# Seven products of halves in place of eight, for two blocks of the gate and up product of each feed-forward layer

## The chip, the core and the metric

The kernel runs on one NeuronCore of a Trainium2 chip, as one launch. The metric is device time in microseconds (us): the median of the timed executions of the whole program. The core has five engines with a queue each: PE (TensorE, matrix products into PSUM), DVE (VectorE), ACT (ScalarE), POOL (GpSimd) and SP (SyncE, which issues the loads). Each works off its own instructions in the order in which the program lists them, and waits on semaphores for the others.

## The reference

A two-layer encoder for 256 tokens of width 1024 in fp32. Each layer is a feed-forward block, a mixer, and a second feed-forward block, all with RMSNorm ahead of them; so there are four feed-forward blocks (FFN) with two different mixers between them. The part that the change touches is the first product of each FFN:

```python
def swiglu(h, w_gu, w_down):
    g, u = jnp.split(h @ w_gu, 2, axis=-1)
    return (jax.nn.silu(g) * u) @ w_down

x = x + 0.5 * swiglu(rmsnorm(x, ffn1_norm[l]), ffn1_w_gu[l], ffn1_w_down[l])
```

Here h is 256 x 1024, w_gu is 1024 x 5632 (2816 gate columns and 2816 up columns) and w_down is 2816 x 1024.

## The kernel before, in words

**Precision.** Every fp32 operand of a product is split into two fp32r halves, hi (the rounded value) and lo (the rest), and a product is three matmul terms: hi by hi, hi by lo, lo by hi. The activations are split once (`xs`, lines 567 and 576-579). The weights are split as they come in: `fetch` (480-498) loads 1 MB (128 x 2048 fp32) into one of RAW = 4 buffers `raw`, and for each of its two parts of 1024 columns ACT copies it to `hi` (`E.copy`, which the planner may give to DVE) and DVE subtracts, `lo = raw - hi`. The parts live in a ring of RING = 6 pairs of hi and lo buffers: a part can be split only when the PE is done with the part six before it. 1024 columns of 128 rows are here called a **part**, of 1 MB two.

**The FFN** (`ffn`, 656-695). The 2816 hidden columns are 22 tiles of 128. A **pass** (672-679) computes two tiles: their two gate and two up products over K = 1024 in eight steps, 32 calls of `wide` (182-187), with the weights stationary and the 256 tokens moving. One `wide` is a matmul of 512 moving columns (both halves of the activations against hi) and one of 256 (their hi half against lo). A pass uses four parts of weights and 64 matmuls, into four PSUM banks, and 11 passes make the gate and up product. `evac` (661-669) then empties each tile's two banks: it adds the halves, multiplies by the row of 1/rms (`rb`), applies SiLU, multiplies gate by up, and splits the result into `hs`, tile by tile: for each tile 3 ACT copies or activations and a split, and on DVE four 256-wide instructions besides a 512-wide one. `hs` is the moving operand of the down product (682-695), with eight output tiles over 22 steps.

**The order of the work.** The program is recorded as a list of operations and put in order by a planner (`schedule`, 162-272), which keeps a clock for each engine, uses written costs (lines 308, 312, 318-321, 340), and of the operations that are ready on an engine takes the one with the lowest priority number. That number is the PE time recorded so far less a lead: 10e3 ns for weight splits (`LEAD_W`), 20e3 for evacuations (`LEAD`), 30e3 for loads (line 485). The resulting order is fixed in the program. In the profile nearly every instruction therefore has one line, that of the planner's emitter (L285 before, L289 after).

Of the kernel before, what the change touches and what calls it, by code (L numbers as in the profile page):

```python
# [14 lines left out]
AF = mybir.ActivationFunctionType  # L15
ALU = mybir.AluOpType
# [3 lines left out]
P = 128  # L20
# [18 lines left out]
LEAD, LEAD_A, LEAD_W = 20e3, 20e3, 10e3  # L39
PATIENCE = 500.0  # L40
WARM = 8


GC = {"norm": 0, "cq": 48, "bs": 51, "sub": 59, "mq": 60, "mk": 61}
# [307 lines left out]
def trunk_kernel(ctx: ExitStack, tc: tile.TileContext, a: dict, out: bass.AP):  # L352
# [108 lines left out]
    def load(ap, widths):  # L461

        o, ids = 0, []
        for w in widths:
            pieces.append((len(loads), o, w))
            ids.append(len(pieces) - 1)
            o += w
        loads.append((ap, o))
        return ids

    def first(raw, w, n):

        for k in range(4):
            o = NGC + (4 * n + k) * N
            c = slice(o if o > NGC else 0, o + N)
            Q.dma_start(out=gx[:, c], in_=a["gx"][:, c])
            c = slice(512 * k, 512 * k + 512)
            Q.dma_start(out=raw[:, c], in_=w[:, c])

    def fetch(n):  # L480
        while len(ready) <= min(n, len(pieces) - 1):
            d, o, w = pieces[len(ready)]
            while len(raws) <= d:
                ap, wide = loads[len(raws)]
                raw = raws_(SUB)
                with lead(30e3):
                    if len(raws) < 2:
                        first(raw, ap, len(raws))
                    else:
                        Q.dma_start(out=raw[:, :wide], in_=ap)  # L490
                raws.append(raw)
            hi, lo = his(PIECE), los(PIECE)
            cuts = 1 if len(ready) > 3 else 2
            with lead(LEAD_W):
                for c in (slice(z * w // cuts, (z + 1) * w // cuts) for z in range(cuts)):
                    E.copy(out=hi[:, c], in_=raws[d][:, o:o + w][:, c])
                    V.tensor_tensor(out=lo[:, c], in0=raws[d][:, o:o + w][:, c], in1=hi[:, c], op=ALU.subtract)
            ready.append((hi, lo))

    def weight(i):  # L500
        fetch(i)
# [41 lines left out]
    def dense(b, xh, xl, wh, wl, first, last):  # L543

        with prog.together():
            c = 0.0
            for l, r, s, e in ((xh, wh, first, False), (xh, wl, False, False), (xl, wh, False, last)):
                c += T.matmul(b, lhsT=l, rhs=r, start=s, stop=e)
# [20 lines left out]
    rr = [rr_[:, h:h + 1] for h in range(2)]  # L569

    def gains(n, j, w, k):

# [8 lines left out]
    def squares(k):  # L581

        if k == 0:
            S.activation(out=acc, in_=x[:, k, :], func=AF.Square)
            return
        sq = t1(N)
        S.activation(out=sq, in_=x[:, k, :], func=AF.Square)
        V.tensor_tensor(out=acc, in0=acc, in1=sq, op=ALU.add)

    def normed(n, k):  # L590

        scaled(n, k)
        squares(k)

    def rms():

# [56 lines left out]
    def finish(k):  # L653
        Q.dma_start(out=out[:, k, :], in_=x[:, k, :])

    def ffn(gu, dn, after):
        hs = Arena(region)(FT, 2, N)
        with lead(LEAD):
            rms_along()

        def evac(j, g, u):
            h, sg = t2(2, N), t1(N)
            for i, b in enumerate((g, u)):
                E.copy(out=h[:, i, :], in_=b[:, 1, :])
                V.tensor_tensor(out=h[:, i, :], in0=b[:, 0, :], in1=h[:, i, :], op=ALU.add)
            V.tensor_tensor(out=h, in0=h, in1=rows(rb, 2), op=ALU.mult)
            S.activation(out=sg, in_=h[:, 0, :], func=AF.Silu)
            V.tensor_tensor(out=sg, in0=sg, in1=h[:, 1, :], op=ALU.mult)
            split(hs[:, j, 0, :], hs[:, j, 1, :], sg)


        for j in range(0, FT, 2):
            banks = [bank(2, N) for _ in range(4)]
            for k in range(KT):
                for t in range(4):
                    wide(banks[t], *chunk(gu, 16 * j + 4 * k + t), xs[:, k], k == 0, k == KT - 1)
# [339 lines left out]


    def ffn_loads(i):
        gu = [n for s in range(FT) for n in load(a["gu"][i, s], (1024, 1024))]
        dn = [n for s in range(FT // 2) for n in load(a["dn"][i, s], (1024, 1024))]  # L1020
        return gu, dn

# [26 lines left out]
        for k in range(KT):  # L1049
            squares(k)  # L1050
    setup()
    ffn(*f10, norm[1])
    even(ev_in, ev_out, norm[2])
    ffn(*f20, norm[3])
    ffn(*f11, norm[4])
    odd(od_in, od_out, norm[5])
    ffn(*f21, finish)
    prog.emit(tc)


# [12 lines left out]

def _gate_up(w):

    return _chunks(w.reshape(KT, P, 2, FT // 2, 2, P).transpose(3, 0, 4, 2, 1, 5))


def _down(w, last):
# [78 lines left out]
```

## Time and profile before

| | |
|---|---|
| median of 3 timed runs | 947.79 us (947.37 to 948.18) |
| the profiled execution's own time | 947.75 us |
| its span in the trace | 946.0 us |
| PE, DVE, ACT busy share of the span | 99%, 77%, 58% |
| first FFN's gate and up product | from 5.26 us to 130.34 us |
| second FFN's gate and up product | starts at 288.27 us |
| bytes read from HBM | 165.86 MB |

How to read it: the trace is of one execution. Rows of a timeline give the start in us, the duration in us, the engine, and the operation with its operands by the program's names. Where the next instruction of an engine starts before the duration of the one ahead has passed, the two overlap in the engine's pipeline; the distance from start to start is then what an instruction costs in a queue that is never empty. A group row gives the count, the busy time and the mean duration, then the idle time of the engine just ahead of these instructions and what ended it.

### The profile page before, as it was taken

The page shows a single profiled execution, that of the slowest core. Times are in us where ns is not written, and L with a number is a line of the kernel's source. Part 1 is how long each engine was busy: PE and PEld are TensorE (multiplying, and loading weights), DVE is VectorE, ACT ScalarE, POOL GpSimd, SP SyncE. Part 2 cuts the span into 40 slices and gives each one's busy share as a digit, 9 for nine tenths or more (in the row PEclk, how much of TensorE's full clock was granted, in tenths as well). Part 3 has the DMA queues.
Part 4 walks back from the last instruction along what each step waited for, and adds up shares of the span by engine and source line. Part 5 has one row for each costly group of instructions (what it writes and reads, how often), then busy time and mean ns, then how long its engine had stood idle before and what let it go on. Part 6 is the DMA issues. An engine that isn't in the chain of part 4 may idle for free.

```text
span 946.0 us, 14528 instructions
## 1 busy us (share of the span) xinstructions
PE 939.6 (99%) x5564; PEld 827.1 (87%) x5564; DVE 724.0 (77%) x1326; ACT 548.4 (58%) x938; POOL 29.4 (3%) x57
## 2 busy tenths in 40 slices
PE   9999999999999999999999999999999999999998
PEld 8888888888899888888888888888989988888887
DVE  7997776579989878866588887756888698887642
ACT  7765655446856656554465656544587566565430
POOL 0920000000000000000000000000000000000000
PEclk9999999999999999999999999999999999999999
DMA  8675555543355555555555555554412355555520
GB/s 334 258 267 178 188 201 191 178 178 134 106 207 177 184 193 203 178 182 191 195 182 187 185 202 192 178 185 162 178 55 85 110 186 196 180 192 205 191 102 22
DMA packets 26422, 167.83 MB, mean 177 GB/s; under 512 B 2929, under 2 KB 5105, under 8 KB 7025
## 3 DMA queue, kind: packets, MB, share of 16 engines
q1 hardware_dynamic: 26352, 166.92, 50.0%
q8 instruction: 43, 0.70, 0.3%
q14 instruction: 27, 0.21, 0.1%
HBM read 165.86 MB, written 1.05 MB: 176 GB/s over the span
## 4 chain that ended last, share of the span: by engine, by line
PE 97%; DVE 1%; ACT 1%; DMA 0%; issue 0%; SPq 0%; ACTq 0%
PE bank L285 97%; DVE t L285 0%; ACT t L285 0%; DMA raw<-in_gu 0%; DVE sm L285 0%; ACT hi L285 0%; DVE region L285 0%; DVE lo L285 0%; ACT L285 0%; DVE hi L285 0%; DVE ssg L285 0%; DVE gx L285 0%; SPq L285 0%; DVE ssc L285 0%; DVE rc L285 0%
## 5 line engine op out<-in xcount | busy, mean ns | idle before, releaser
L285 DVE TENSOR_TENSOR lo<-raw,hi 128x1024 fp32r<-128x1024 f32 (+2 forms) x318 | 382.4, 1204 | 165.9 <-ACT hi L285 161.0
L285 ACT ACTIVATE hi<-raw 128x1024 fp32r<-128x1024 f32 (+3 forms) x310 | 322.6, 1043 | 306.1 <-PE bank L285 193.2
L285 PE MATMUL bank<-xs,hi 128*128 128x512 f32 x1408 | 490.8, 393 | 0.4 <-ACT hi L285 0.4
L285 PE MATMUL bank<-xs,lo 128*128 128x256 f32 x1408 | 394.8, 280 | 0.0
L285 PEld LDWEIGHTS bank<-xs,hi 128*128 128x128 f32 x1408 | 265.4, 189 | 59.1 <-ACT hi L285 0.7
L285 PE MATMUL bank<-region,hi 128*128 128x512 f32 (+1 forms) x982 | 296.6, 364 | 0.0
L285 PEld LDWEIGHTS bank<-xs,lo 128*128 128x128 f32 x1408 | 265.3, 188 | 0.7 <-DVE lo L285 0.7
L285 PE MATMUL bank<-region,lo 128*128 128x256 f32 x832 | 234.0, 281 | 0.0
L285 PEld LDWEIGHTS bank<-region,hi 128*128 128x128 f32 x982 | 174.9, 189 | 32.0
L285 PEld LDWEIGHTS bank<-region,lo 128*128 128x128 f32 x832 | 157.6, 189 | 0.0
L285 ACT ACTIVATE t<-bank 128x256 f32<-128x256 f32 (+1 forms) x201 | 76.5, 400 | 39.4 <-PE bank L285 38.4
L285 PE MATMUL bank<-hi,xs 128*128 128x512 f32 (+2 forms) x256 | 78.6, 381 | 0.0
L285 DVE TENSOR_TENSOR t<-bank,t 128x256 f32<-128x256 f32 x176 | 67.3, 420 | 0.4 <-ACT t L285 0.4
L285 DVE TENSOR_TENSOR t<-t,rb 128x512 f32<-128x512 f32 x88 | 60.3, 689 | 1.2
L285 PEld LDWEIGHTS bank<-hi,xs 128*128 128x128 f32 x256 | 47.1, 188 | 8.7
L285 DVE SCALAR_TENSOR_TENSOR gx<-bank,gx 128x256 f32<-128x256 f32 (+1 forms) x71 | 28.4, 450 | 28.7 <-PE bank L285 28.6
L285 PE MATMUL bank<-lo,xs 128*128 128x512 f32 (+2 forms) x128 | 48.0, 375 | 0.0
L285 DVE TENSOR_TENSOR t<-t,t 128x256 f32<-128x256 f32 (+2 forms) x108 | 45.9, 428 | 0.1
L285 ACT ACTIVATE t<-t 128x256 f32<-128x256 f32 (+2 forms) x98 | 39.0, 406 | 3.1 <-DVE t L285 3.1
L285 DVE TENSOR_TENSOR region<-t,region 128x256 fp32r<-128x256 f32 (+2 forms) x92 | 39.1, 430 | 1.1 <-ACT region L285 1.1
L285 ACT ACTIVATE region<-t 128x256 fp32r<-128x256 f32 (+1 forms) x89 | 35.5, 404 | 1.6 <-DVE t L285 1.4
L285 ACT ACTIVATE xs<-gx 128x256 fp32r<-128x256 f32 x48 | 24.0, 500 | 10.8 <-DVE gx L285 9.7
(129 smaller groups left out, 467.4 us busy)
## 6 DMA issues: line engine op xcount, KB each, us to landing
raw<-in_gu SPq DMA_DIRECT2D x86, 1024.0 KB, 4.8
raw<-in_dn SPq DMA_DIRECT2D x44, 1024.0 KB, 4.8
raw<-in_ev_in SPq DMA_DIRECT2D x10, 1024.0 KB, 4.8
raw<-in_ev_out SPq DMA_DIRECT2D x4, 1024.0 KB, 4.9
raw<-in_od_out SPq DMA_DIRECT2D x4, 1024.0 KB, 4.7
raw<-in_gu SPq DMA_DIRECT2D x8, 256.0 KB, 4.6
raw<-in_od_q SPq DMA_DIRECT2D x2, 1024.0 KB, 5.0
raw<-in_od_c SPq DMA_DIRECT2D x2, 832.0 KB, 4.3
```

The lines of the kernel that those rows point to most:

```text
L285: r = fn(*map(real, args), **{k: real(v) for k, v in kw.items()})
```

## The change

Of the 22 tiles, eight are no longer computed in passes of two but in two **S blocks** of four tiles each, behind the third pass: `PLAN = "P P P S S P P P P"`. In an S block the operands trade places: the activations are stationary (128 tokens) and 512 weight columns move. With the tokens in two halves and K in two halves of four steps each, gate and up of four tiles (512 columns each) are a 2 x 2 by 2 x 2 block product, done in Winograd's form of Strassen's algorithm by seven products of halves. Each is four K steps by three 512-wide matmuls (`dense`).

- **Weights.** The four 1 MB quarters b11, b12, b22, b21 are loaded, and four sums are formed on DVE from the raw fp32 values: b11 + b12, b12 + b22 (in place, in the raw buffer), b11 plus that, and that plus b21. As each 1 MB is handled in two parts, this is eight DVE additions of 128 x 1024. Then fourteen parts (seven operands of two) are split into hi and lo, where the four tiles had eight parts in two passes.
- **Activations.** `row_sums` forms four differences or sums of scaled activations, once for each FFN, in four groups, and splits them; it is recorded behind the first pass, with the lead of the weight splits. The second rms (`rms()`, for the tokens as partitions) is computed once for each FFN too.
- **Evacuation.** The products accumulate in three banks, with copies and additions between them; gate and up come out with tokens as partitions, so that eight transposes on the PE turn the result for `hs`.

The core of the diff:

```diff
+PLAN = "P P P S S P P P P"
+    def load_sums(aps):
+        b11, b12, b22, b21 = range(len(loads), len(loads) + 4)
+        loads.extend((ap, SUB) for ap in aps)
+        def plus(out, a, b):
+            V.tensor_tensor(out=out, in0=a, in1=b, op=ALU.add)
+            return out
+        part = lambda d, o: loaded(d)[:, o:o + PIECE]
+        scratch = lambda z, o: sums_[:, z, o:o + PIECE]
+        def s2(o):
+            s1 = plus(part(b12, o), part(b12, o), part(b22, o))
+            return plus(scratch(1, o), part(b11, o), s1)
+        ids = []
+        for of in (b11, lambda o: plus(scratch(0, o), part(b11, o), part(b12, o)), s2, b22, b12, b21,
+                   lambda o: plus(scratch(1, o), scratch(1, o), part(b21, o))):
+            ids.append(range(len(pieces), len(pieces) + 2))
+            pieces.extend((of, o, PIECE) for o in (0, PIECE))
+        return ids
...
+    def row_sums(n, j):
+        xg, f = t2(4, P), t2(4, P)
+        for i, k in enumerate((j, j + KT // 2)):
+            E.scaled(xg[:, 2 * i:2 * i + 2, :], x[:, k, :].rearrange("p (h n) -> p h n", h=2), gcol[:, 8 * n + k:8 * n + k + 1])
+        V.tensor_tensor(out=f[:, 0:2, :], in0=xg[:, 0:4:3, :], in1=xg[:, 1:2, :].broadcast_to([P, 2, P]), op=ALU.subtract)
+        V.scalar_tensor_tensor(out=f[:, 2, :], in0=f[:, 1, :], scalar=-1.0, in1=xg[:, 0, :], op0=ALU.mult, op1=ALU.subtract)
+        V.scalar_tensor_tensor(out=f[:, 3, :], in0=xg[:, 2, :], scalar=-1.0, in1=f[:, 2, :], op0=ALU.mult, op1=ALU.subtract)
+        split(sf[:, 0, j], sf[:, 1, j], f)
...
+        def four(ids, j):
...
+            product(a, x_(0, 0), 0, first=True)
+            p1 = copied(a)
+            product(c, f_(1), 1, first=True)
+            p5 = copied(c)
+            product(a, f_(2), 2)
+            u2 = copied(a)
+            product(c, f_(3), 3)
+            with lead(LEAD):
+                V.tensor_tensor(out=u2, in0=c, in1=u2, op=ALU.add)
+            product(a, f_(0), 4)
+            with lead(LEAD):
+                V.tensor_tensor(out=p5, in0=a, in1=p5, op=ALU.add)
+            product(b, x_(4, 0), 5, first=True)
+            with lead(LEAD):
+                V.tensor_tensor(out=p1, in0=b, in1=p1, op=ALU.add)
+                S.activation(out=p1, in_=p1, func=AF.Silu, scale=rr[0])
+            h0 = gated(0, p1, u2)
+            product(a, x_(4, 1), 6)
...
-        for j in range(0, FT, 2):
+        j = 0
+        for ids in gu:
+            if len(ids) == 7:
+                four(ids, j)
+                j += 4
+                continue
...
+            if j == 0:
+                with lead(LEAD_W):
+                    for i in range(KT // 2):
+                        row_sums(n, i)
+            j += 2
```

Two places show what this does to DVE's queue. In the rows, `raw` are the loaded weights, `hi` and `lo` the ring, `t1` and `t2` scratch tiles, `region32` the scratch of the weight sums, `region` the place of `hs` and of the split row sums, `bank` PSUM. The first place is the start of the first FFN on DVE, where the weights of the second pass are split (`lo4_122<-raw2_110`, its first part). Before:

```order
L285 TENSOR_TENSOR acc_149<-acc_149,t1_5_66 128x256
L285 TENSOR_TENSOR acc_149<-acc_149,t1_0_61 128x256
L285 CAST hi5_117<-raw2_110 128x1024
L285 TENSOR_TENSOR lo4_122<-raw2_110,hi4_116 128x1024
L285 TENSOR_TENSOR acc2_150<-acc_149,acc2_150 128x256
```

That split stands two rows behind the last sum of squares (`acc`). Of the changed kernel, the same split with what is in front of it:

```order
L289 TENSOR_TENSOR region_132<-t2_5_72,region_132 128x512
L289 SCALAR_TENSOR_TENSOR rb_148<-t1_2_63,rb_148 128x256
L289 SCALAR_TENSOR_TENSOR t2_8_75<-t2_2_69,t2_8_75 128x128
L289 TENSOR_TENSOR t2_6_73<-t2_6_73,rb_148 128x512
L289 TENSOR_TENSOR t2_7_74<-t2_7_74,rb_148 128x512
L289 TENSOR_REDUCE nlam_166<-t1_4_65 128x2
L289 TENSOR_TENSOR region_132<-t2_8_75,region_132 128x512
L289 TENSOR_TENSOR t2_0_67<-t2_4_71 128x256
L289 TENSOR_TENSOR lo4_122<-raw2_110,hi4_116 128x1024
```

It now stands at row 69, where it stood at row 28: behind the row sums (`t2_8_75`, `region_132`), the two rsqrt chains (`rb`) and the first pass's evacuation. The second place is the middle of the second FFN's gate and up product on DVE. Before, a pass there reads:

```order
L285 TENSOR_TENSOR lo0_118<-raw1_109,hi0_112 128x1024
L285 TENSOR_TENSOR t2_4_71<-bank0_124,t2_4_71 128x256
L285 TENSOR_TENSOR t2_4_71<-bank4_128,t2_4_71 128x256
L285 TENSOR_TENSOR t2_7_74<-bank7_131,t2_7_74 128x256
L285 TENSOR_TENSOR t2_4_71<-t2_4_71,rb_148 128x512
L285 TENSOR_TENSOR lo1_119<-raw1_109,hi1_113 128x1024
L285 TENSOR_TENSOR t1_0_61<-t1_0_61,t2_4_71 128x256
L285 TENSOR_TENSOR t2_7_74<-bank6_130,t2_7_74 128x256
L285 TENSOR_TENSOR t2_7_74<-t2_7_74,rb_148 128x512
L285 TENSOR_TENSOR lo2_120<-raw2_110,hi2_114 128x1024
```

Between two weight splits (`lo`) stand a few 256-wide and 512-wide rows. Where the first S block ends and the second begins there now stands:

```order
L289 TENSOR_TENSOR lo1_119<-raw1_109,hi1_113 128x1024
L289 SCALAR_TENSOR_TENSOR t2_2_69<-t2_2_69,nrr_151,t2_8_75 128x512
L289 TENSOR_TENSOR region32_133<-raw1_109,raw2_110 128x1024 x2
L289 TENSOR_TENSOR region_132<-bank2_126,region_132 128x2x256
L289 TENSOR_TENSOR region_132<-bank4_128,region_132 128x2x256
L289 TENSOR_TENSOR lo2_120<-region32_133,hi2_114 128x1024
L289 TENSOR_TENSOR lo3_121<-region32_133,hi3_115 128x1024
L289 TENSOR_TENSOR raw2_110<-raw2_110,raw3_111 128x1024 x2
L289 TENSOR_TENSOR region32_133<-raw1_109,raw2_110 128x1024 x2
L289 TENSOR_TENSOR lo0_118<-raw3_111,hi0_112 128x1024
L289 TENSOR_TENSOR lo4_122<-region32_133,hi4_116 128x1024
```

The 1024-wide rows now stand in rows of their own, six of them sums of weights, and the splits `lo2`, `lo3`, `lo4` read what these sums leave in `region32`.

More of the change, by code (lines that the diff above doesn't have):

```diff
@@ L478, in first, with loaded @@
             Q.dma_start(out=raw[:, c], in_=w[:, c])
+    def loaded(d):
+        while len(raws) <= d:
+            ap, wide = loads[len(raws)]
+            raw = raws_(SUB)
+            with lead(30e3):
+                if len(raws) < 2:
+                    first(raw, ap, len(raws))
+                else:
+                    Q.dma_start(out=raw[:, :wide], in_=ap)
+            raws.append(raw)
+        return raws[d]
     def fetch(n):
@@ L482, in fetch @@
             d, o, w = pieces[len(ready)]
[L483 to L491, printed above, removed]
             hi, lo = his(PIECE), los(PIECE)
@@ L541, in split, with dense @@
             V.scalar_tensor_tensor(out=dst_lo, in0=src, scalar=gain, in1=dst_hi, op0=ALU.mult, op1=ALU.subtract)
-    def dense(b, xh, xl, wh, wl, first, last):
+    def dense(b, xh, xl, wh, wl, first, last, more=False):
         with prog.together():
@@ L547, in dense @@
             for l, r, s, e in ((xh, wh, first, False), (xh, wl, False, False), (xl, wh, False, last)):
-                c += T.matmul(b, lhsT=l, rhs=r, start=s, stop=e)
+                c += T.matmul(b, lhsT=l, rhs=r, start=s, stop=e, skip_group_check=more)
         prog.clock += c
@@ L568, in trunk_kernel @@
     rr_, rb, acc, acc2 = keep("rr", 2), keep("rb", N), keep("acc", N), keep("acc2", 2, N, dt=F32R)
-    rr = [rr_[:, h:h + 1] for h in range(2)]
+    rr, nrr = [rr_[:, h:h + 1] for h in range(2)], keep("nrr", 2)
     def gains(n, j, w, k):
@@ L659, in ffn, with product, copied, gated @@
             rms_along()
+            rms()
+            V.tensor_scalar(out=nrr, in0=rr_, scalar1=-1.0, scalar2=None, op0=ALU.mult)
+        def four(ids, j):
+            x_ = lambda k, h: lambda z, i: xs[:, i + k, z, half(h)]
+            f_ = lambda n: lambda z, i: sf[:, z, i, n, :]
+            a, b, c = bank(512), bank(512), bank(512)
+            def product(bk, rows_, n, first=False):
+                for i in range(4):
+                    hi, lo = weight(ids[n][i // 2])
+                    w = slice(i % 2 * 512, i % 2 * 512 + 512)
+                    dense(bk, rows_(0, i), rows_(1, i), hi[:, w], lo[:, w], first and i == 0, i == 3, not first)
+            def copied(bk):
+                t = t2(512)
+                with lead(LEAD):
+                    E.copy(out=t, in_=bk)
+                return t
+            def gated(h, sg, s):
+                with lead(LEAD):
+                    V.scalar_tensor_tensor(out=s, in0=s, scalar=nrr[:, h:h + 1], in1=sg, op0=ALU.mult, op1=ALU.mult)
+                return s
+            product(a, x_(0, 0), 0, first=True)
[8 more added lines that the diff above has]
+            product(a, f_(0), 4)
+            with lead(LEAD):
+                V.tensor_tensor(out=p5, in0=a, in1=p5, op=ALU.add)
+            product(b, x_(4, 0), 5, first=True)
+            with lead(LEAD):
+                V.tensor_tensor(out=p1, in0=b, in1=p1, op=ALU.add)
+                S.activation(out=p1, in_=p1, func=AF.Silu, scale=rr[0])
+            h0 = gated(0, p1, u2)
+            product(a, x_(4, 1), 6)
+            with lead(LEAD):
+                sg = t2(512)
+                S.activation(out=sg, in_=a, func=AF.Silu, scale=rr[1])
+            h1 = gated(1, sg, p5)
+            with lead(LEAD):
+                for i in range(0, 4, 2):
+                    tp = aux(2, 2, P)
+                    with prog.together(50.0):
+                        for z in range(2):
+                            for h, t in enumerate((h0, h1)):
+                                T.transpose(tp[:, z, h, :], t[:, (i + z) * P:(i + z + 1) * P], ident)
+                    tp = tp.rearrange("p z h n -> p z (h n)")
+                    split(hs[:, j + i:j + i + 2, 0, :], hs[:, j + i:j + i + 2, 1, :], tp)
@@ L1018, in ffn_loads @@
     def ffn_loads(i):
-        gu = [n for s in range(FT) for n in load(a["gu"][i, s], (1024, 1024))]
+        gu, o = [], 0
+        for z in PLAN.split():
+            aps = [a["gu"][i, o + s] for s in range(2 if z == "P" else 4)]
+            gu.append(load_sums(aps) if z == "S" else [n for ap in aps for n in load(ap, (1024, 1024))])
+            o += len(aps)
         dn = [n for s in range(FT // 2) for n in load(a["dn"][i, s], (1024, 1024))]
@@ L1074, in _gate_up @@
 def _gate_up(w):
-    return _chunks(w.reshape(KT, P, 2, FT // 2, 2, P).transpose(3, 0, 4, 2, 1, 5))
+    r, j = [], 0
+    for z in PLAN.split():
+        if z == "P":
+            r.append(_chunks(w.reshape(KT, P, 2, FT, P)[:, :, :, j:j + 2].transpose(0, 3, 2, 1, 4)))
+        else:
+            t = w.reshape(2, 4, P, 2, DFF)[..., j * P:(j + 4) * P]
+            r += [t[k, :, :, c].transpose(1, 0, 2).reshape(1, P, SUB) for k, c in ((0, 0), (0, 1), (1, 1), (1, 0))]
+        j += 2 if z == "P" else 4
+    return np.concatenate(r)
 def _down(w, last):
```

20 lines of the change are left out of this document (12 added, 8 removed).

## The prediction, made before the run

> **What bounds the kernel now.** I read the page first: the shares of the engines, then the chain that ended last.
>
> ```profile
> PE 939.6 (99%) x5564; PEld 827.1 (87%) x5564; DVE 724.0 (77%) x1326; ACT 548.4 (58%) x938; POOL 29.4 (3%) x57
> PE 97%; DVE 1%; ACT 1%; DMA 0%; issue 0%; SPq 0%; ACTq 0%
> ```
>
> 97% of the chain is the PE, so work taken from the PE is time, as long as nothing else takes its place. Next in line is DVE, with 77% as an average over stages. The change works in the gate and up stages, so the stage is what counts: busy time of the engines (in the order PE, weight load, DVE, ACT) in a steady stretch of the first of them, and the DVE queue in it.
>
> ```profile
> 90.00:110.00 20.00, 20.00 (x117) 17.62 (x116) 15.65 (x25) 12.31 (x23) 0.00 (x0) 1.00 0.58 204
> ...
> 95.51 1.23 DVE L285 TENSOR_TENSOR lo<-raw,hi 128x1024 fp32r<-128x1024 f32 x1 [1.20 <-ACT hi L285]
> 96.65 1.10 DVE L285 TENSOR_TENSOR t<-bank,t 128x256 f32<-128x256 f32 x3
> 97.67 0.68 DVE L285 TENSOR_TENSOR t<-t,rb 128x512 f32<-128x512 f32 x1
> 98.29 1.23 DVE L285 TENSOR_TENSOR lo<-raw,hi 128x1024 fp32r<-128x1024 f32 x1
> ...
> 106.60 1.23 DVE L285 TENSOR_TENSOR lo<-raw,hi 128x1024 fp32r<-128x1024 f32 x1 [1.20 <-ACT hi L285]
> ```
>
> A pass takes 106.60 - 95.51 = 11.09 us. From start to start a DVE row costs 96.65 - 95.51 = 1.14 us at 1024 wide, (97.67 - 96.65) / 3 = 0.34 at 256 and 98.29 - 97.67 = 0.62 at 512. That is 0.28 us for 256 more columns and a fixed 0.06, so by estimate 0.20 at 128 and some 0.07 for the tiny ones. A pass gives DVE 4 splits of weights, 8 rows of 256 and 2 of 512: 4.6 + 2.7 + 1.2 = 8.5 us of 11.09. So DVE has 2.6 us to spare in a pass, a quarter, and no more.
>
> **What the PE gains.** The pace of the two kinds of matmul streams, and of transposes:
>
> ```profile
> 288.27 0.39 PE L285 MATMUL bank<-xs,hi 128*128 128x512 f32 x1
> ...
> 288.62 0.39 PE L285 MATMUL bank<-xs,hi 128*128 128x512 f32 x1
> ...
> 195.08 0.63 PE L285 MATMUL bank<-hi,xs 128*128 128x512 f32 x2
> ...
> 195.78 0.63 PE L285 MATMUL bank<-hi,xs 128*128 128x512 f32 x2
> ...
> 696.90 1.35 PE L285 MATMUL bank<-ident,t 128*128 128x128 f32 x8
> 698.00 0.47 PE L285 MATMUL bank<-hi,region 128*128 128x512 f32 x1
> ```
>
> A `wide` takes 0.35 us (32 of them make the 11.09); three 512-wide matmuls of the mixers' form, which is that of an S block, take 0.70, so one takes 0.233. Four tiles were two passes, 22.2 us. An S block is 7 products x 12 = 84 matmuls, 19.6 us, and 8 transposes, 1.1 us: 20.7. The PE is spared 1.5 us in each of the 8 S blocks, 12 us in all.
>
> **What DVE must do for it.** An S block gives DVE 14 splits and 8 sums of 1024, 22 x 1.14 = 25.1 us; 5 rows of 512 in its evacuation, 3.1; and 2 of 512 with a scalar by partition. Their price: the row with such a scalar below takes 0.40 at 256 where the plain one takes 0.34, so 0.68 at 512, 1.4 for two.
>
> ```profile
> 285.62 0.48 DVE L285 SCALAR_TENSOR_TENSOR xs<-gx,xs 128x256 fp32r<-128x256 f32 x1
> 286.02 0.42 DVE L285 TENSOR_TENSOR acc<-acc,t 128x256 f32<-128x256 f32 x1
> 286.36 0.68 DVE L285 SCALAR_TENSOR_TENSOR gx<-bank,gx 128x512 f32<-128x512 f32 x1
> ```
>
> That is 29.6 us of DVE against 20.7 of PE. DVE becomes the bound in the S blocks. The trace before shows no sum of weights; I take the split's 1.14, since both read two fp32 tensors of 1024 from SBUF and write one, and the row that adds two fp32 scratch tiles (`acc`, 0.34 at 256) fits the same line. ACT has 14 copies, 14.8 us by the mean below, and 7 rows of 512 in the evacuation, by estimate 0.6 to 0.7 each, half a copy and its fixed part: some 19 us, far from DVE's 29.6.
>
> ```profile
> L285 ACT ACTIVATE hi<-raw 128x1024 fp32r<-128x1024 f32 x294 | 311.0, 1060 | 295.2 <-PE bank L285 186.2 <-issue 103.2 <-ACT hi L285 2.7
> ```
>
> **How much of it shows.** The lead that DVE can build is six parts of weights, and the order fixes what stands in the queue. In the second FFN I count, in the order of the changed kernel, from the first row of the second pass's evacuation to the split of the last part of the second S block: 29 splits and 16 sums of 1024 (45 x 1.14 = 51.3), 16 rows of 256 (5.4), 12 of 512 (7.4), 3 with a scalar (2.0): 66.0 us. The third and fourth FFN have the same rows, the first has one cast more, of 17.68 - 17.08 = 0.6 (its like is in the rows on the first FFN, below). The queue is in order, so this stretch can't be shorter. Going through it with the PE's and ACT's times I find DVE waiting only twice, for ACT's copy of a sum, some 0.4 us each: 0.8. Behind the last split the PE still has half a product (6 x 0.233 = 1.4), the transposes (1.1) and four passes less the 8 matmuls that it does while waiting (44.4 - 1.4 = 43.0): with 0.1 for the semaphore, 45.6 us.
>
> What comes ahead of that stretch: row sums and the second rms, some 6 us of DVE (4 x 0.34, 8 x 0.20, 4 x 0.62, 8 tiny rows), recorded so that they come before the splits of later parts. The rows for the second FFN, where the PE begins at 288.27:
>
> ```profile
> 289.55 0.68 DVE L285 SCALAR_TENSOR_TENSOR gx<-bank,gx 128x512 f32<-128x512 f32 x1
> ...
> 310.30 1.10 DVE L285 TENSOR_TENSOR t<-bank,t 128x256 f32<-128x256 f32 x3
> ```
>
> Before, the second pass's evacuation begins 22.0 us behind the PE's start. In the changed kernel DVE must wait for two small products that the PE does between the first pass's matmuls, the later of them after 46 matmuls, at 8.6 us; behind it stand 7 splits (8.0), 18 rows of 256 (6.1), 4 of 512 (2.5), 4 of 128 (0.8) and the tiny ones (0.5), 17.8 us. The evacuation begins at 26.4. In between the PE waits about 3 us for the second pass's second part. Sum: 26.4 + 66.0 + 0.8 + 45.6 = 138.8 us from the PE's start, where 11 passes and the rms product took 122.3: **+16.5**. The fourth FFN, also behind a mixer, has the same rows: **+16.5**. The third follows a down product, and most of its row sums stand ahead of the end of that; 22.3 us of rows from 0.3 on: 22.6 + 66.0 + 0.8 + 45.6 = 135.0, **+12.7**.
>
> The first FFN has no stage ahead in which to split:
>
> ```profile
> 5.26 211.39 PE bank L285 x1165
> ...
> 15.29 1.87 DVE L285 TENSOR_TENSOR acc<-acc,t 128x256 f32<-128x256 f32 x4
> 17.08 0.69 DVE L285 CAST hi<-raw 128x1024 fp32r<-128x1024 f32 x1
> 17.68 1.22 DVE L285 TENSOR_TENSOR lo<-raw,hi 128x1024 fp32r<-128x1024 f32 x1
> ...
> 31.11 0.41 DVE L285 TENSOR_TENSOR t<-bank,t 128x256 f32<-128x256 f32 x1
> ...
> 130.34 0.39 PE L285 MATMUL bank<-region,hi 128*128 128x512 f32 x1
> ```
>
> From the sums of squares at 15.29 on, 46 rows, 13.1 us, stand ahead of the second pass's first split, and a wait of 0.8 for the first pass's bank. So that split ends at 30.3 and the PE, done with the first pass at 130.34 - 10 x 11.09 = 19.4, stands still for some 11 us. The second pass then ends at 41.6 and its evacuation begins at 41.2, where 31.11 was its first row before. 41.2 + 66.6 + 0.8 + 45.6 = 154.2, where the down product began at 130.34: **+23.9**.
>
> Together +69.6. The loads are not in it: a raw buffer falls free when its sums and splits are done, and the second S block's quarters, by the same count, have 10 us or more from there to their first use, where a load of 1 MB takes under 5:
>
> ```profile
> raw<-in_gu SPq DMA_DIRECT2D x86, 1024.0 KB, 4.8
> ```
>
> Nothing is given back later: behind the S blocks the passes run at the PE's pace. The profiled run took 947.75 us, 1.75 more than its span and within 0.04 of the median, so the forecast is 947.75 + 69.6 = 1017 us.
>
> **The rivals.**
>
> *DVE keeps up and the PE's saving shows* (the other side). Then the time is 947.75 - 12 = 936 us. For that, DVE's 22 rows of 1024 would have to fit into 20.7 - 4.5 = 16.2 us, 0.74 us each, and the row sums into the spare 2.6 us of the passes. From 0.74 on it turns; 1.14 speaks against it. What speaks for it is only that no sum of two raw fp32 tensors was seen. Chance 2%; that it comes out even, 1%.
>
> *Only the S blocks show, the start is hidden.* If DVE begins the stretch where it did before (22.0), because row sums fall into waits that I counted twice or go to ACT, each FFN gives 22.0 + 66.0 + 45.6 - 122.3 = 11.3 us: 947.75 + 45 = 993. Against it: the order puts the row sums ahead of the splits. 13%.
>
> *The PE slows down after standing still.* The first stretch of the run shows it, with the PE's count in 4.74 us and in the 10 us that follow:
>
> ```profile
> 5.26:10.00 4.74, 4.74 (x14) 3.72 (x15) 4.34 (x9) 4.37 (x10) 0.00 (x0) 1.00 0.95 320
> 10.00:20.00 10.00, 10.00 (x59) 8.88 (x58) 9.24 (x20) 7.71 (x18) 0.00 (x0) 1.00 1.00 405
> ```
>
> 14 matmuls in 4.74 us is half of the later pace (59 in 10), though the granted clock reads 1.00: 2.4 us lost. If it comes back after each long halt (11 us in the first FFN, some 3 in the second and fourth, and one of some 4 us in the second S block of all four), it is up to 7 x 2.4 = 17 us: 1034. The halts in the S blocks are cheap, as the PE has some 2 us to spare there behind them. 22%. [...]
>
> *Each DVE row costs its full duration* (1.23 where I took 1.14; 0.42 for 0.34; 0.68 for 0.62). Then the stretch is 45 x 0.09 + 16 x 0.08 + 15 x 0.06 = 6.2 us longer, the time 1017 + 25 = 1042. [...] The rows at 95.51 and 96.65 show it otherwise, so 1%.
>
> **How the numbers follow.** The main case has 61%: 1017, for itself 1008 to 1027, as the waits of DVE are known to a few us in each FFN. I take 998 to 1036 as the range, which holds the main case and the slow clock, and leaves out the hidden start and the two ends. Faster by over 0.2% (about what a measurement of this kernel can tell from no change): 2%; within: 1%; slower: 97%.
>
> **What would show it.** In the profile after: the chain is no longer 97% PE but goes through DVE's `lo` and `region32` in four stretches; DVE is busy without a gap for some 66 us in each gate and up product; the weight sums take 1.14 us from start to start; the PE stands still for about 11 us near 20 us; passes behind the S blocks take 11.1 us as before. Wrong would be the forecast if the sums cost under 0.8 us, if DVE shows gaps inside the S blocks, or if the down products or the mixers became longer.

## The result, and the profile after

| | before | after |
|---|---|---|
| median | 947.77 us (947.37 to 948.18) | 1033.84 us (1032.04 to 1036.33) |
| ratio to before | | 1.0907, 95% interval 1.0891 to 1.0923 |
| profiled execution, span | 947.75, 946.0 | 1032.04, 1030.3 |
| first FFN's gate and up product ends at | 130.34 | 157.71 (27.4 later) |
| second: length | 122.28 | 142.80 (+20.5) |
| third | 122.27 | 138.55 (+16.3) |
| fourth | 122.28 | 142.41 (+20.1) |

The changed kernel is slower by 86 us; the forecast was 1017, with a range of 998 to 1036. A length in the table runs from the PE's first matmul on `xs` to its first of the down product. The four excesses add up to 84.3 us, the difference of the two spans. Outside these stages nothing moved: from the end of the first to the start of the second it is 157.94 us, where it was 157.93.

The page of the changed kernel: the line of engines, the granted clock in 40 slices, and the chain by engine.

```profile
PE 964.8 (94%) x5292; PEld 818.8 (79%) x5292; DVE 843.5 (82%) x1444; ACT 605.1 (59%) x956; POOL 29.8 (3%) x57
PEclk8898999999999998999999899999999999999999
PE 79%; DVE 15%; ACT 4%; issue 1%; DMA 0%; SPq 0%; ACTq 0%; DVEq 0%
```

The PE has 272 matmuls fewer (5564 before), but is counted busy for 25 us more. Its share of the chain fell from 97% to 79%, and DVE's rose from 1% to 15%. DVE has 119.5 us more to do. The row of the clock has slices under 9, which look ahead to the part that the forecast had too small.

The timeline of DVE in the second FFN, from the first row of the second pass's evacuation, over the sums of weights, to the last split of the second S block (at 411.76) and the row behind it, the first split of the next pass (columns: start, duration, operation, and in brackets the idle time ahead and what ended it):

```profile
343.16 1.18 DVE L289 TENSOR_TENSOR t<-bank,t 128x256 f32<-128x256 f32 x3 [0.66 <-ACT t L289]
...
389.42 2.36 DVE L289 TENSOR_TENSOR raw<-raw,raw 128x1024 f32<-128x1024 f32 x2
391.69 2.36 DVE L289 TENSOR_TENSOR region<-raw,raw 128x1024 f32<-128x1024 f32 x2
393.96 1.23 DVE L289 TENSOR_TENSOR lo<-raw,hi 128x1024 fp32r<-128x1024 f32 x1
...
402.49 0.69 DVE L289 TENSOR_TENSOR t<-bank,t 128x512 f32<-128x512 f32 x1 [1.35 <-PE bank L289]
...
411.76 1.22 DVE L289 TENSOR_TENSOR lo<-region,hi 128x1024 fp32r<-128x1024 f32 x1
412.90 1.22 DVE L289 TENSOR_TENSOR lo<-raw,hi 128x1024 fp32r<-128x1024 f32 x1
```

A sum costs (393.96 - 391.69) / 2 = 1.135 us, the 1.14 that was assumed. The stretch runs from 343.16 to 412.90, 69.7 us. It holds the rows that were counted (29 splits, 16 sums, 16 rows of 256, 12 of 512, 3 with a scalar: 66.0 us). That leaves 3.7 us, where the forecast had 0.8 for waits. The view by windows has DVE busy for 66.56 us of it (its third pair of numbers, behind PE and weight load), so DVE stands idle for 3.2:

```profile
343.16:412.90 69.74, 59.37 (x245) 44.80 (x244) 66.56 (x77) 43.42 (x58) 0.00 (x0) 0.93 0.40 145
```

The PE's timeline at both ends of this stage:

```profile
315.65 0.39 PE L289 MATMUL bank<-xs,hi 128*128 128x512 f32 x1
...
458.45 0.39 PE L289 MATMUL bank<-region,hi 128*128 128x512 f32 x1
```

The evacuation begins 343.16 - 315.65 = 27.5 us in (forecast 26.4), and 458.45 - 412.90 = 45.55 us follow the last split (forecast 45.6). So 142.8 = 27.5 + 69.7 + 45.6, where 138.8 was forecast. Over all four FFN the stages are 14.7 us longer than forecast: the stretch gives some 11 of them (2.3 to 3.3 in each), the start 3.5. In the first FFN the forecast halt of some 11 us is there too:

```profile
30.30 0.58 PE L289 MATMUL bank<-xs,lo 128*128 128x256 f32 x1 [10.72 <-DVE lo L289]
```

The window behind it has a granted clock of 0.50, with 8 matmuls in 2.71 us where the steady pace is 59 in 10:

```profile
30.00:33.00 3.00, 2.71 (x8) 2.34 (x9) 3.00 (x7) 0.81 (x2) 3.00 (x7) 0.50 0.00 0
```

What the forecast lacked shows in the PE's rows behind the halts of the S blocks. Here the second FFN, with x2 for two matmuls in a row:

```profile
360.00 0.39 PE L289 MATMUL bank<-hi,region 128*128 128x512 f32 x1
362.26 0.50 PE L289 MATMUL bank<-hi,region 128*128 128x512 f32 x1 [1.86 <-ACT hi L289]
364.16 0.50 PE L289 MATMUL bank<-lo,region 128*128 128x512 f32 x1 [1.40 <-DVE lo L289]
...
367.02 1.05 PE L289 MATMUL bank<-hi,region 128*128 128x512 f32 x2
367.88 0.59 PE L289 MATMUL bank<-lo,region 128*128 128x512 f32 x1
368.30 0.62 PE L289 MATMUL bank<-hi,region 128*128 128x512 f32 x2
368.75 0.39 PE L289 MATMUL bank<-lo,region 128*128 128x512 f32 x1
...
393.50 0.50 PE L289 MATMUL bank<-hi,region 128*128 128x512 f32 x1 [0.69 <-ACT t L289]
395.24 0.53 PE L289 MATMUL bank<-lo,region 128*128 128x512 f32 x1 [1.24 <-DVE lo L289]
395.58 1.04 PE L289 MATMUL bank<-hi,region 128*128 128x512 f32 x2
396.42 0.63 PE L289 MATMUL bank<-lo,region 128*128 128x512 f32 x1
...
399.23 0.63 PE L289 MATMUL bank<-hi,region 128*128 128x512 f32 x2
399.70 0.39 PE L289 MATMUL bank<-lo,region 128*128 128x512 f32 x1
```

From 364.16 to 368.30 ten matmuls of 512 take 4.1 us, and from 395.24 to 399.23 ten take 4.0: some 0.40 each. From 399.23 on three take 0.70, the 0.233 of before. Each such phase costs the PE 1.7 us; a third one lies between them, behind halts of 0.97 and 1.20 us, from 388.43 on. The windows give the granted clock beside it (the number ahead of the DMA share):

```profile
364.00:372.00 8.00, 7.28 (x23) 5.08 (x23) 8.00 (x8) 2.53 (x4) 0.00 (x0) 0.79 0.71 264
395.00:403.00 8.00, 7.76 (x27) 6.23 (x28) 6.47 (x7) 3.90 (x5) 0.00 (x0) 0.79 0.76 260
```

DVE's wait of 1.35 us at 402.49 is for the PE, shortly behind the last of these phases.

### The profile page after: what moved, and what is told of

It reads as the page before. It is cut to its first block, busy times and chain, and to the rows that moved or that the text cites. A ratio compares the mean times of both kernels' runs of the same rounds, so it can differ in the third digit from the quotient of the medians.

```text
span 1030.3 us, 14056 instructions
## 1 busy us (share of the span) xinstructions
PE 964.8 (94%) x5292; PEld 818.8 (79%) x5292; DVE 843.5 (82%) x1444; ACT 605.1 (59%) x956; POOL 29.8 (3%) x57
## 4 chain that ended last, share of the span: by engine, by line
PE 79%; DVE 15%; ACT 4%; issue 1%; DMA 0%; SPq 0%; ACTq 0%; DVEq 0%
PE bank L289 79%; DVE lo L289 6%; DVE region L289 4%; DVE t L289 4%; ACT hi L289 2%; ACT t L289 1%; DVE raw L289 1%; DMA gx<-in_gx 0%; DVE sm L289 0%; ACT xs L289 0%; DVE rb L289 0%; ACT region L289 0%; SPq L289 0%; DVE hi L289 0%; ACT L289 0%
## 5 line engine op out<-in xcount | busy, mean ns | idle before, releaser
L289 ACT ACTIVATE hi<-raw 128x1024 fp32r<-128x1024 f32 (+2 forms) x313 | 324.0, 1041 | 277.8 <-PE bank L289 214.7
L289 PE MATMUL bank<-xs,hi 128*128 128x512 f32 x896 | 317.8, 397 | 0.1
L289 PE MATMUL bank<-xs,lo 128*128 128x256 f32 x896 | 253.9, 283 | 17.9 <-DVE lo L289 17.3
L289 PEld LDWEIGHTS bank<-xs,hi 128*128 128x128 f32 x896 | 170.7, 191 | 37.7 <-ACT hi L289 0.4
L289 PEld LDWEIGHTS bank<-xs,lo 128*128 128x128 f32 x896 | 170.8, 191 | 21.5 <-DVE lo L289 21.3
L289 PE MATMUL bank<-hi,xs 128*128 128x512 f32 (+2 forms) x448 | 143.6, 389 | 1.7 <-ACT hi L289 1.7
L289 PE MATMUL bank<-hi,region 128*128 128x512 f32 (+1 forms) x280 | 107.4, 451 | 15.9 <-ACT hi L289 9.5
L289 PEld LDWEIGHTS bank<-hi,region 128*128 128x128 f32 x280 | 61.8, 221 | 36.5 <-ACT hi L289 12.5
L289 PE MATMUL bank<-lo,region 128*128 128x512 f32 (+1 forms) x140 | 64.1, 458 | 16.7 <-DVE lo L289 16.7
L289 DVE TENSOR_TENSOR t<-bank,t 128x256 f32<-128x256 f32 (+1 forms) x136 | 60.2, 468 | 12.1 <-ACT t L289 6.4
L289 PEld LDWEIGHTS bank<-lo,xs 128*128 128x128 f32 x224 | 42.2, 188 | 20.5 <-DVE lo L289 13.6
L289 ACT ACTIVATE hi<-region 128x1024 fp32r<-128x1024 f32 x47 | 49.1, 1055 | 15.8 <-DVE region L289 15.8
```

Of the source, the lines that this page charges most:

```text
L289: r = fn(*map(real, args), **{k: real(v) for k, v in kw.items()})
```

## The experiments

The theory: in each gate and up product DVE is one full queue from the start of the stage to the last split of the last S block, and the PE is paced by it. The rivals are in each expectation. In the diffs a line that is only "..." marks what is left out. Where no interval is given a kernel was run once, beside the kernel before on the same chip (947.6, 948.3, 947.7 or 950.6 us).

### The sums of the weights: left out, and doubled in part

```diff
-            V.tensor_tensor(out=out, in0=a, in1=b, op=ALU.add)
-            return out
+            return b
```

> The eight sums of weights of each S block are left out (the products read a raw quarter in their place, so this computes something else); splits, products, transposes and row sums stay. Theory (DVE's queue bounds the S blocks): DVE's rows of an S block fall from 29.6 to 20.5 us, under the PE's 20.7, so the S blocks run at the PE's pace and save 12 us, while the halts at the start of the gate and up stages stay (11.3 us in the first FFN, 3.2 in the second and fourth, and about 4 for the slow clock behind them): 947.8 - 12 + 22 = 958 us, 950 to 966. Rival (the transposed form of the products is slow by itself, or PE waits for ACT's copies between the products): the S blocks stay longer than 25 us each, over 1000 us.

Measured: 957.19 us. The first stage ends 9.8 us later than before, the second is 1.6 longer, the third 3.5 shorter, the fourth 1.5 longer. Without the sums nine tenths of the loss are gone, with the seven products, the splits and the row sums still there. The third stage shows the PE's saving for the first time: 3.5 us for two blocks, where 1.5 for each was forecast.

In the second kernel the sums b11 + b12 and b11 + (b12 + b22) are done twice: eight more rows of 1.14 us in a stage.

```diff
-        def plus(out, a, b):
+        def plus(out, a, b, twice=False):
             V.tensor_tensor(out=out, in0=a, in1=b, op=ALU.add)
+            if twice:
+                V.tensor_tensor(out=out, in0=a, in1=b, op=ALU.add)
...
-            return plus(scratch(1, o), part(b11, o), s1)
+            return plus(scratch(1, o), part(b11, o), s1, True)
...
-        for of in (b11, lambda o: plus(scratch(0, o), part(b11, o), part(b12, o)), s2, b22, b12, b21,
+        for of in (b11, lambda o: plus(scratch(0, o), part(b11, o), part(b12, o), True), s2, b22, b12, b21,
```

> Four of the eight sums of each S block (b11 + b12, and b11 plus the second sum, two parts each) are done twice, with the same result. Theory: DVE is never idle there, so all 8 x 1.14 = 9.1 us of each FFN show: 1033.8 + 36.5 = 1070 us, 1065 to 1076. Rival (DVE is not the bound, or the slow clock of the PE is): the additions find room, under 1045 us.

Measured: 1059.89 us, 26 of the 36.5 us that were added, below the expected range: 6.5 to 7.3 in a stage in place of 9.1. DVE is the bound, but not without a gap: in the second FFN the added rows fill part of the waits in the stretch (3.2 us in the changed kernel, 2.3 here), and one row with a scalar (0.66) has moved behind the last split. The wait of 1.35 us for the PE, for one, has only one of 0.23 as its like here.

### The row sums, recorded later

They are recorded with the third pass in place of the first, alone and without the sums of weights.

```diff
-            if j == 0:
+            if j == 4:
                 with lead(LEAD_W):
```

> The row sums are recorded in the third pass in place of the first, so the planner puts the weight splits of the second pass ahead of them; nothing else changes. Theory: the halt of 11 us in the first FFN goes, and those of 3 us in the second and fourth; DVE does the row sums in the 2.6 us that each pass leaves: 1033.8 - 12 - 2 x 4.5 - 1 = 1012 us, 1006 to 1020. Rival (that work only moves into the stretch in which DVE is full): 1028 us or more.

Measured: 1031.86 us, no change beside the changed kernel's 1032.04 to 1036.33; the rival was right. The timeline of the PE in the first FFN shows why:

```profile
49.32 0.79 PE L289 MATMUL bank<-lo,xs 128*128 128x512 f32 x1 [6.13 <-DVE lo L289]
```

The halt at 30 us is gone, and one of 6.13 us has come up in front of the first S product. What DVE saves early it owes later, as it has no slack up to the last split.

> No weight sums, as in the first run, and the row sums and the second rms are recorded ahead of the third pass, as in the third run. The output differs by the sums. Theory (row sums cost wherever they stand only as long as DVE is full): with 20.5 us of DVE in an S block of 20.7 the queue has 2.6 us to spare in each pass behind the blocks only, so the halt of the first FFN goes (10.7 us) and some 3 in the second and fourth: 940 us (934 to 949), below the kernel before. Rival, their place never matters: 957 as without the move.

Measured: 945.84 us. With the sums out DVE has room, and now the same move is worth 957.19 - 945.84 = 11.3 us. So the place of the row sums matters only where DVE is not the bound. The time lies in the range of the theory. With the sums left out the kernel is 2.5 us under the one before (948.3 on that chip), 0.3% between single runs. It isn't the limit of what the PE's saving could bring: the second to fourth stage are 1.9, 3.4 and 1.7 us shorter than before, but the first is 5.4 longer, with a halt of the PE of 7.0 us ahead of its first S product. No order without that halt was run.

### No S blocks, one, and the blocks elsewhere

```diff
-PLAN = "P P P S S P P P P"
+PLAN = "P P P P P P P P P P P"
```

> All 22 tiles in passes; the row sums and the second rms are computed as in the changed kernel, and not used. Theory: what is left is the start of the stages alone: 947.8 + 11.3 + 2 x 3.2 + about 4 for the slow clock behind the halts = 969 us, 962 to 975. Rival (the row sums only cost where S blocks follow): 950 us or less.

Measured: 973.22 us, in the range of the theory. The row sums and the second rms, which nobody reads here, cost 25 us: 12.8 in the first FFN, 6.7, 0.45 and 5.5 in the others.

```diff
-PLAN = "P P P S S P P P P"
+PLAN = "P P P S P P P P P P"
```

> One S block in each gate and up product, with nine passes, in place of two blocks and seven. Theory (DVE is one full queue from the start of the stage to the last split of the last S block, and only passes follow): the start stays (evacuation of the second pass 27.5 us in), the stretch loses a whole block, 69.8 - 29.6 - about 2 of waits = 38, and 45.6 + 22.2 = 67.8 follow; 133.3 us in the second FFN where two blocks take 142.8, so 9.5 less in each of the four: 1033 - 38 = 994 us (986 to 1002). Rival, the start is a price of its own and the rest goes by the block (973 without S blocks, 1033 with two): 1003. Rival, the cost lies where two S blocks meet: below 980.

Measured: 995.14 us. The forecast of the queue, 994, was met; the rival by the block (1003) was not.

```diff
-PLAN = "P P P S S P P P P"
+PLAN = "P P S P P S P P P"
```

> The two S blocks stand apart: two passes, S, two passes, S, three passes. The work is the same. Theory (one full DVE queue up to the last split): one pass more stands ahead of the last split (8.5 us of DVE), one less behind it (11.1 of the PE), so 2.6 us less in each of the four: 1022 us (1014 to 1031). Rival, the lead of six parts is built anew in the two passes between the blocks and pays twice (two passes spare 5.2 us of DVE, and a lead is worth 6.8): 1005 to 1012. Rival, each block costs the same wherever it stands: 1032 or more.

Measured: 1018.21 us. The same work in another order is 15.6 us shorter than 1033.84, 3.9 in a stage, where the queue alone gives 2.6. What the rest of it is stays open.

```diff
-PLAN = "P P P S S P P P P"
+PLAN = "P P P P S P P S P"
```

> The two S blocks stand as late as the order of passes allows without being last: four passes, S, two passes, S, one pass. The work is the same. Theory (one DVE queue that is full from the start of the stage to the last split): three passes more ahead of the last split (8.5 us of DVE each) and three less behind it (11.1 of the PE each), 2.6 us less per pass and stage by the rows, 3.9 by what the run with the blocks apart gave: 4 x 3 x 2.6 to 3.9, so 1033.8 - 31 to 47 = 987 to 1003. The stage can't come under DVE's whole work in it, 27.5 + 69.8 + 4 x 8.5 = 131 us where the kernel before takes 122.3: by this theory no order of the passes comes under about 980. Rival, what helped in the run with the blocks apart was only the lead between them, and more passes behind are worth nothing: 1015 to 1020.

Measured: 1004.25 us, just above the upper end of the theory's range and far from the rival. In this kernel the row sums lie where the passes between the blocks put `hs`, so that its second S block is computed with other operands; the work is the same. The order with two passes at the end has no such overlap:

```diff
-PLAN = "P P P S S P P P P"
+PLAN = "P P P S P P S P P"
```

> Three passes, S, two passes, S, two passes: the last S block ends with two passes to go, where the changed kernel has four, the run with the blocks apart three and the late one a single pass. The work is the same, and the row sums keep their place. Theory (one DVE queue full up to the last split, each pass moved ahead of it is worth 2.6 to 3.9 us in a stage, 2.4 by the late run): 1033.8 - 4 x 2 x (2.4 to 3.9) = 1003 to 1015. Rival, the late run's gain came from tokens' row sums being overwritten there or from the lead between the blocks alone: 1016 to 1020, as with the blocks apart.

Measured: 1007.20 us, inside the range of the theory. Down to two passes behind it, the later the last split, the less is lost. From two passes to one it is only 3 us where the theory has 10, and against the kernel before on its own chip both orders are 6.0% longer (947.7 and 950.6 us there): that the last move helps at all isn't shown. With two blocks each order that was run stays above the kernel before by 56 us or more.

### The sums on GpSimd

```diff
-            V.tensor_tensor(out=out, in0=a, in1=b, op=ALU.add)
+            G.tensor_tensor(out=out, in0=a, in1=b, op=ALU.add)
```

> The 16 weight sums of a gate and up product go to GpSimd. DVE is then as free as in the run without sums (957). The trace has one GpSimd sum of 128x128, 2.21 us in the kernel before and 0.47 in the changed one, so a sum of 128x1024 is by estimate between 8 x 0.47 = 3.8 and 17.6 us, and the 16 take 60 to 280 us of GpSimd in a stage of 122. Theory at the lower end: GpSimd's 30 us for a block are as long as DVE's were, but begin at the start of the stage and stand in a queue of their own: 965 to 1000. At the upper end each stage takes over 280 us: above 1600. If DVE's rows become longer beside GpSimd's (both read SBUF), the 128x1024 split takes over 1.3 us.

Measured: 1070.45 us, between the two ends of the theory and worse than with the sums on DVE. The largest group of GpSimd's rows, with their mean duration in ns:

```profile
L289 POOL TENSOR_TENSOR region<-raw,raw 128x1024 f32<-128x1024 f32 x32 | 96.1, 3023 | 672.1 <-DMA raw<-in_gu 672.1
```

GpSimd's timeline in the second FFN, two sums in a row:

```profile
407.25 6.13 POOL L289 TENSOR_TENSOR region<-raw,raw 128x1024 f32<-128x1024 f32 x2
```

And DVE's beside it and behind it:

```profile
407.76 3.37 DVE L289 TENSOR_TENSOR lo<-region,hi 128x1024 fp32r<-128x1024 f32 x1
411.06 3.41 DVE L289 TENSOR_TENSOR lo<-raw,hi 128x1024 fp32r<-128x1024 f32 x1
414.39 1.27 DVE L289 TENSOR_TENSOR region<-bank,region 128x512 fp32r<-128x512 f32 x2
415.59 2.34 DVE L289 TENSOR_TENSOR lo<-region,hi 128x1024 fp32r<-128x1024 f32 x2
```

A sum takes some 3.0 us on GpSimd, under the lower bound of 3.8. But the two splits on DVE beside these two sums take 3.4 us each, and the two that begin in GpSimd's pause (413.4 to 416.9) 1.13 each. DVE is relieved of 1.14 us for each sum, and each of the two splits beside them costs it 2.2 us more.

### Spare matmuls in the PE's halts

Is the PE's slow clock what lies between 1017 and 1034? Two kernels give the PE something to do in the halts: for each weight part of an S block the first matmul, which needs `hi` alone, is issued two more times, into a bank that nobody reads.

```diff
-    def dense(b, xh, xl, wh, wl, first, last, more=False):
+    def dense(b, xh, xl, wh, wl, first, last, more=False, idle=None):
...
                 c += T.matmul(b, lhsT=l, rhs=r, start=s, stop=e, skip_group_check=more)
+                if idle is not None and r is wh and l is xh:
+                    for _ in range(2):
+                        T.matmul(idle, lhsT=l, rhs=r, start=True, stop=True)
...
-            a, b, c = bank(512), bank(512), bank(512)
+            a, b, c, idle = bank(512), bank(512), bank(512), bank(512)
...
-                    dense(bk, rows_(0, i), rows_(1, i), hi[:, w], lo[:, w], first and i == 0, i == 3, not first)
+                    dense(bk, rows_(0, i), rows_(1, i), hi[:, w], lo[:, w], first and i == 0, i == 3, not first, idle if i % 2 == 0 else None)
```

> The changed kernel with two more matmuls of 512 columns for each weight part of the S blocks, put behind the first matmul on that part (which needs only hi), so that they run where the PE otherwise stands and waits for lo. Their results go to a bank that nobody reads. They are 8 x 14 x 2 = 224 matmuls, 52 us of the PE. Theory (DVE sets the S blocks, the PE has 8.9 us to spare in each, and its slow clock after a halt costs only some us of DVE's waits): the 52 us vanish, 1028 to 1040. Rival, the PE's slow clock after its halts is what lies between the forecast 1017 and the measured 1033.8: the PE, never standing for long, keeps its clock and the time falls to 1017 to 1024. Rival, the PE sets part of the S blocks: 1045 to 1086.

Measured: 1036.99 us, ratio 1.0945 (1.0927 to 1.0963), in the theory's range. But the trace says that this number hides two effects. The evacuation of the second pass and the last split of the second FFN on DVE:

```profile
344.25 1.08 DVE L289 TENSOR_TENSOR t<-bank,t 128x256 f32<-128x256 f32 x3
...
408.30 1.22 DVE L289 TENSOR_TENSOR lo<-region,hi 128x1024 fp32r<-128x1024 f32 x1
```

The stretch is 408.30 + 1.14 - 344.25 = 65.2 us, 4.5 less than in the changed kernel. From there to the down product at 460.22 it is 50.8 us, 5.2 more: the 52 us of spare matmuls were too many, and at the end the PE is late. That left the clock open, so the next kernel puts spare matmuls only into the first three products of each block. Of its diff, the line that differs from the kernel just shown:

```diff
+                    dense(bk, rows_(0, i), rows_(1, i), hi[:, w], lo[:, w], first and i == 0, i == 3, not first, idle if n < 3 and i % 2 == 0 else None)
```

> As the run with spare matmuls, but only in the first three products of each S block, where the trace of the changed kernel has the PE's halts and its slow matmuls behind them (0.42 us each for some 3.5 us): 12 spare matmuls in a block, 2.8 us, none behind. In the run with spare matmuls throughout, DVE's stretch in the second FFN was 65.2 us in place of 69.7, and the work behind the last split 50.8 in place of 45.6, so that what DVE gained the busier PE lost. Theory A (DVE's waits of 3.6 us in the stretch come from the PE's slow clock and go with it): the stretch is 65 to 67 us, the rest stays 45.6, 3 to 4.6 us less in each stage: 1015 to 1022. Theory B (the waits are handed on between DVE, ACT and the PE whatever the clock, or the spare matmuls push the PE back as before): 1030 to 1038, with the stretch over 68.5 us or the rest over 48.

Measured: 1017.99 us (1016.94 to 1018.23), ratio 1.0740 (1.0725 to 1.0755): 15.8 us faster than the changed kernel, with 96 matmuls more. The time, the stretch and the rest lie where theory A had them. DVE's stretch in the second FFN, and its busy time in it:

```profile
340.22 1.18 DVE L289 TENSOR_TENSOR t<-bank,t 128x256 f32<-128x256 f32 x3 [0.65 <-ACT t L289]
...
405.22 1.23 DVE L289 TENSOR_TENSOR lo<-region,hi 128x1024 fp32r<-128x1024 f32 x1
...
340.22:406.36 66.14, 60.16 (x269) 47.17 (x268) 65.40 (x75) 42.10 (x57) 0.00 (x0) 0.97 0.39 144
```

The two windows that had a granted clock of 0.79 in the changed kernel, and one between them, where a slow phase is left:

```profile
364.00:372.00 8.00, 8.00 (x37) 6.58 (x36) 8.00 (x9) 4.41 (x6) 0.00 (x0) 1.00 0.77 293
386.66:390.07 3.41, 3.41 (x9) 2.16 (x7) 3.41 (x4) 2.00 (x2) 0.00 (x0) 0.50 0.00 0
395.00:403.00 8.00, 7.90 (x35) 6.13 (x35) 8.00 (x9) 5.00 (x6) 0.00 (x0) 1.00 0.83 329
```

The stretch is 405.22 + 1.14 - 340.22 = 66.1 us, DVE's idle time in it is 0.7 us in place of 3.2, and the work behind the last split is 451.83 - 406.36 = 45.5. The S blocks of the second FFN have one slow phase in place of three, and the mean granted clock of the whole run is 0.984, where it was 0.969. But the two kernels differ in more than that. With the fourth bank and the spare matmuls the planner puts rows of DVE and ACT in another order at several places of this FFN, and one row with a scalar (0.66 us) now stands behind the last split. Of the idle time that is gone, the 1.35 us for the PE stood shortly behind a slow phase. The rest were waits for ACT, and two of them, 0.5 us at 360.50 and 362.54, stood ahead of the first slow phase in the S blocks, which therefore can't have made them. How much of the 15.8 us is the clock and how much the order is not separated: no kernel was run with the bank and the new order but without the spare matmuls.

## Why the prediction was right, and where it was too low

- **DVE becomes the bound in the S blocks: right.** The sum costs 1.135 us (1.14 taken), the rows in the stretch are the ones counted, and taking the sums out removes 77 of the 86 us.
- **The PE is spared 1.5 us by a block: right.** Without the sums, the third FFN is 3.5 us shorter than before, where 3.0 was forecast; with the sums all of it is covered by DVE.
- **Behind the last split, 45.6 us: right** (45.55). No run shows the 0.1 us for the semaphore in it by itself; in the trace of the changed kernel a matmul that waits for a split starts 0.05 us behind its end (395.24, where the split at 393.96 lasts 1.23). Nothing came back later: down products and mixers are unchanged.
- **The start: 1.1 us too small.** 27.5 in place of 26.4 us to the evacuation in the second FFN, where the PE halts for 3.19 us and then runs at a granted clock of 0.50 from 334.15 to 337.57; in the third, which has no such halt, it is 22.9 in place of 22.6. In the first the PE's halt ended at 30.30, as forecast, but the second pass's evacuation began at 42.4 in place of 41.2, as the pass ran at a granted clock of 0.50 at first. That the place of the row sums in the order sets the cost was not borne out: recorded later, they cost the same, since DVE has no slack up to the last split.
- **Waits of DVE in the stretch, 0.8 us: this step failed.** DVE is idle for 3.2 us in the second FFN, and the stretch is 2.9 longer than forecast. The prediction put it: "The halts in the S blocks are cheap, as the PE has some 2 us to spare there behind them." They are not. Behind halts of 0.7 to 1.9 us in pairs the granted clock was 0.50 for 3.4 us, which cost the PE 1.7 us each time, three times in the second FFN; and since DVE's evacuation rows stand in the same queue as the splits, a late PE or a late copy of its bank holds up the splits behind them. One wait, of 1.35 us for the PE, is seen shortly behind such a phase; that the others come from the clock is not shown.
- **The rival of the slow clock (1034, 22%) came true in size, partly by luck.** Its sum was 2.4 us for each of up to seven long halts. The halt of 11 us and the two of 3 are there, but none of the four of some 4 us; short halts in pairs stood in their place, and a slow phase cost 1.7 us. That 1034 and 1033.84 lie so close is chance. What was measured is 15.8 us less when the PE is kept busy in most of its halts, in a somewhat different order of rows. With that, the kernel takes 1017.99 us, and its stages exceed those before by 24.4, 16.8, 12.1 and 17.1 us, where 23.9, 16.5, 12.7 and 16.5 had been forecast. The totals of the forecast are met there, in part because errors cancel: in the second FFN the start is still 27.5 us, 1.1 more than forecast, and the stretch 0.7 less, as one row has left it.
- **DVE keeps up (936): wrong.** Even with the sums left out, the fastest kernel that was run took 945.84 us.
- **Rows at their full duration (1042): wrong.** Rows of 1024 start 1.135 us apart, though each lasts 1.22.

The prediction named gaps of DVE inside the S blocks as a sign against itself. They are there, 5% of the stretch, and are most of what the forecast was short of.

## What to carry to other kernels

An algorithm with fewer products pays with operand sums on another engine, so set these sums and the extra splits against that engine's spare time in the same stage before counting the saving: here 12 us of the PE were bought with 64 sums and 48 more splits, of 1.14 us each, on an engine that had 2.6 us to spare in 11. Where one engine's queue is full from the start of a stage to a certain row, the order in front of that row moves halts but not the end; only less work in that queue helps, or more of the other engine's work in front of that row (1033.8, 1018.2, 1007.2 and 1004.3 us with four, three, two and one passes behind it, in single runs but for the first). And once the PE waits often, look at the granted clock: the kernel that fills the PE's halts with useless matmuls has a mean of 0.984 where the changed kernel has 0.969, and is 15.8 us faster, part of which may be the new order of the other queues.

## What the runs showed of the hardware that was not expected

**A granted clock of 0.50 stood behind short halts too.** Behind two halts of 1.86 and 1.40 us with one matmul between them, and behind two of 0.69 and 1.24, ten matmuls took some 0.40 us each in place of 0.233. Both times the granted clock was 0.50 for 3.41 us. The windows of 3.41 us ahead of two such phases, and the phases:

```profile
361.46:364.87 3.41, 1.22 (x4) 0.81 (x5) 3.27 (x4) 2.09 (x3) 0.00 (x0) 1.00 0.00 0
364.87:368.28 3.41, 3.41 (x9) 2.20 (x8) 3.41 (x4) 2.00 (x2) 0.00 (x0) 0.50 0.50 175
...
392.18:395.59 3.41, 1.49 (x6) 0.68 (x5) 3.23 (x4) 2.73 (x4) 0.00 (x0) 1.00 0.15 24
395.59:399.01 3.42, 3.42 (x10) 2.65 (x9) 3.42 (x4) 0.70 (x1) 0.00 (x0) 0.50 0.70 283
```

The prediction had looked for this only behind halts of 3 us and more. In the 3.41 us ahead of these two phases the PE was busy for 1.22 and 1.49 us. The length of a halt alone doesn't tell whether a slow phase comes: in the last kernel with spare matmuls a halt of 2.54 us goes with one in each of the first three FFN (in the second, a granted clock of 0.50 from 386.66 to 390.07), and the like halt of 2.55 us in the fourth with none (three matmuls in 0.70 us behind it).

**DVE's splits took longer beside GpSimd's sums.** In the kernel with the weight sums on GpSimd, two DVE splits with two SBUF operands each took 3.37 and 3.41 us beside two GpSimd sums (6.13 us from 407.25 on), somewhat more than a sum's 3.07; the two that begin in GpSimd's pause (413.4 to 416.9) took 1.13 each. Not every split beside a sum was longer: the one at 394.43 took 1.21 us, with GpSimd at its sums from 393.62 on. What makes the difference isn't shown. One split in the first FFN of this run even lasted 11.57 us:

```profile
52.45 11.57 DVE L289 TENSOR_TENSOR lo<-region,hi 128x1024 fp32r<-128x1024 f32 x1 [4.99 <-ACT hi L289]
```

GpSimd's sums were not of one length either: the one at 375.78 took 2.38 us, the two from 393.62 on 7.60 together, and the mean of the largest group is 3.02. Whether DVE's rows lengthen them isn't shown.
